# Seven products for eight in four row pairs of a down projection

## The chip, the cores and the metric

The kernel runs on one core of a Trainium2 chip. The metric is the device time of one execution in microseconds (us), lower is better. A core has a matrix engine (TensorE, PE in the profile; its loads of the stationary operand are the row PEld), a vector engine (VectorE, DVE), a scalar engine (ScalarE, ACT), a general engine (GpSimd, POOL) and the queue SP, from which most transfers are issued. Each engine runs its instructions in the order in which they were written, and semaphores make it wait for others.

## The reference

One decoder layer on x (512 tokens by 1024): a token mixer, then a gated MLP with a convolution, each followed by a residual sum and a layer norm. The change lies in the last third, the down projection of the MLP and the layer norm behind it:

```python
def conv_ffn(h, w_up, conv_w, conv_b, w_down):
    u = causal_dwconv(h @ w_up, conv_w, conv_b)
    g, val = jnp.split(u, 2, axis=-1)
    return (jax.nn.silu(g) * val) @ w_down          # 512 x 2816 times 2816 x 1024
# in reference():
        y = conv_ffn(h, w_up, conv_w, conv_b, w_down)
        x = layer_norm(DEEPNORM_ALPHA * x + (1.0 + g2) * y, ln2_g, ln2_b)
```

All is float32. `g2` is a row of 1024 gate values, computed from the conditioning vector c.

## The kernel before, in words

**Precision.** Every large product is made from three: a float32 operand is split into a high part (rounded to the matrix engine's faster float32 form, by a copy on ScalarE) and a low part (the rest, by a subtraction on VectorE), and `mm3` (line 464) adds high x high, high x low and low x high into one bank of the accumulation memory. So each weight tile and each activation tile needs one ScalarE copy and one VectorE subtraction before TensorE may use it.

**Order.** The kernel is written as threads (Python generators) that yield operations, buffers (`buf`, `bank`) and conditions (`Need`). A planner, class `Order`, keeps a clock for each engine and a model price for each operation (`price`, line 199); it emits, engine by engine, the operation that can start first, and among those that can start at about the same time the one with the lowest priority number. What it emits is a fixed order for each engine; on the chip only data and buffers make engines wait. Buffers come in classes: `b` (25 of 4 KB per partition: raw weights, their parts, most middle rows), `e` (6 of 8 KB), `h` (2 of 16 KB), `s` (9 of 2 KB) and `ps` (the 8 accumulation banks, 512 columns each). `R.limit` caps how many of a group may be held at once; all instructions are recorded at line 316, where the planner emits them.

**The up projection** already uses seven products for eight in its tiles 2 to 21 (`seven`, line 729, tiles `sP`). It ends at the mark `fin` (line 1826).

**The down projection** (`ffn`, from line 1823) has two halves of 512 output columns. Half n runs over 22 rows of 128 middle values, taken as 11 row pairs; `by_tile` (line 1674) takes one weight item (a row pair, 128 x 2 x 512) after the other, and for each the four token tiles. For each of the two rows and each token tile there is one `mm3` with 128 tokens of a middle row as the stationary operand and 512 columns of weights as the moving one. Half 0 has four accumulation banks; half 1 has five, since the last token tile is cut in two. The last item of half 0 and the last five of half 1 are run tile by tile, so that layer norm can begin with the first tile.

**What feeds it.** `w_load` (line 742) issues the weight loads on SP, at most 3 raw items at a time after `fin`. `w_split` (line 764) splits each into `wh` and `wl`; at most 8 such buffers (group `w2`) are held. The last 11 items, those of half 1, are first multiplied by the gate row (`raw<-raw,RW`, lines 769 to 772), which half 0 gets later, in `ln2`. The priority of `w_split` depends on how many items it is ahead of TensorE (`split_pri`, line 796). `keep` (line 1452) splits middle rows 6 to 21, which the up projection left unsplit in the buffers `KEEP`, into the tiles `MID`; rows 12 to 19 lie in two buffers of class e, the others by pairs in class b. When those two buffers are free, `x_back` (line 1324) loads the normalized rows XN back from memory, and `row_loads` (line 1479) scales them on GpSimd, a multiplication and an addition for each of 8 half rows, for the residual sum.

**Layer norm** (`ln2`, line 1500) runs per token tile: for half 0, the bank times the gate row, added to XN; for half 1, the bank added to XN; then statistics, the normalization, and the stores.

Of the kernel before, what the change touches and what calls it, by code (L numbers as in the profile page):

```python
# [107 lines left out]
class Order:  # L108
# [90 lines left out]
    def price(self, eng, fn, outs, ins, kw):  # L199
# [221 lines left out]
def layer_kernel(  # L421
# [247 lines left out]
    def start_h():  # L669
        for k in range(KC):  # L670
# [69 lines left out]
    RAW, W, wpos, lead = {}, {}, [0, 0], [0.0, 0.0]  # L740

    def w_load():
        yield Need("loads")
# [11 lines left out]
    def sums_seven(j, r1, a11, a21):  # L755
# [5 lines left out]
        QS[j] = q  # L761
        R.mark(("qs", j))

    def w_split():
        yield Need(("hk", KC - 1))
        for i, (shape, _) in enumerate(items):
            yield Need(("raw", i))
            raw = RAW.pop(i)
            if i >= len(items) - NFF // 2:
                yield Need("g2p")  # L770
                g2 = RES["rw"][:, 0, None, HS[1]].to_broadcast([P, 2, 512])
                yield V.tensor_mul(raw, raw, g2)
            if 0 <= i - len(items) + LATE_DN < 2:
                yield Need("fin")
                m = 2 * (i - len(items) + LATE_DN)
                hi, lo = RES["w"][:, m], RES["w"][:, m + 1]
            elif UP0 <= i < UP0 + 2 * NFF and (i - UP0) // 2 in SEVEN:
                if (i - UP0) % 2 == 0:
                    yield Need(("raw", i + 1))
                    yield from split_seven((i - UP0) // 2, raw, RAW[i + 1])  # L780
                R.free(raw)
                wpos[1] = i + 1
                continue
            else:
                own = i >= UP0 + NSPLIT
                hi = yield buf("b", shape, "wh", "w2" if own else "wh", F32R)
                lo = yield buf("b", shape, "wl", "w2" if own else "wl", F32R)
            yield A.activation(hi, raw, AF.Copy)
            yield V.tensor_sub(lo, raw, hi.bitcast(F32))
            R.free(raw)  # L790
            W[i] = (hi, lo)
            wpos[1] = i + 1
            lead[1] += 1
            R.mark(("w", i))
# [657 lines left out]
    def keep():  # L1452

        yield Need("tsused")
        for j in (12, 16):
            KEEP[j] = yield buf("e", [P, 4, SEQ], "keep")
            R.mark(("keep", j))
        yield Need("fin")
        for j in range(NMID, NFF):
            if 12 <= j < 20:  # L1460
                if j % 2 == 0:
                    E8[j] = yield buf("e", [P, 2, 2, SEQ], "mid2", dt=F32R)
                mid = E8[j - j % 2][:, j % 2]
# [6 lines left out]
            R.mark(("mid", j))  # L1470
            n = 4 if 12 <= j < 20 else 2
            if j % n == n - 1:
                R.free(KEEP[j - j % n])
                R.mark(("kfree", j - j % n))
# [4 lines left out]
    def row_loads():  # L1479
# [18 lines left out]
        R.free(*lt, *ab)  # L1498

    def ln2(t, ps, cuts):  # L1500
# [170 lines left out]
    LATE = 4  # L1671
    LATE_DN = 5

    def by_tile(tiles, total, late, block, key, after=None):

        w = {}
        for i in range(total):
            if i < total - late:
                need, n_ = w_next()
                yield Need(need)  # L1680
                w[i] = W.pop(n_)
                for t in tiles:
                    yield from block(i, t, w[i])
                R.free(*w.pop(i))
                if after:
                    after(i)
# [100 lines left out]
    def ffn():  # L1787
# [37 lines left out]
        RES["w"] = yield buf("h", [P, 4, 2, 512], "wlast", dt=F32R)  # L1825
        R.mark("fin")
        R.limit(gemm=8, raw=3, w2=8)
        ps = {}
        cuts = [[(0, 512), (512, DM)]] * 3 + [[(0, 512), (512, 768), (768, DM)]]
        for n in range(2):  # L1830
            for t in range(NT):
                for c in cuts[t][1:] if n else cuts[t][:1]:
                    ps[t, c[0]] = yield bank("gemm", "dn")
                if n == 0:
                    R.spawn(ln2(t, ps, cuts[t]), 0.5 if t == NT - 1 else 1)

            def block(i, tile, w):
                t, (c0, c1) = tile
                s, c = slice(t * P, (t + 1) * P), slice(c0 - n * 512, c1 - n * 512)
                for b in range(2):  # L1840
                    k = 2 * i + b
                    yield Need(("mid", k))
                    yield mm3(ps[t, c0][:, :c1 - c0], MID[k][:, 0, s], MID[k][:, 1, s],
                              w[0][:, b, c], w[1][:, b, c], k == 0, k == NFF - 1)

            tiles = [(t, c) for t in range(NT) for c in (cuts[t][1:] if n else cuts[t][:1])]
            yield from by_tile(tiles, NFF // 2, (1, LATE_DN)[n], block, lambda tile: ("y2", tile[0], tile[1][0]))

    def ada_last():
        yield Need(("item", UP0 - 12))  # L1850
# [30 lines left out]
    R.spawn(products(), lambda: 0.4 if ("hh", 0) in R.done and "b0" not in R.done else 9)  # L1881
    R.spawn(w_load(), 5)
    R.spawn(w_split(), split_pri)
    R.spawn(ada_mid(), lambda: 3 if wpos[0] > 16 else 8)
    R.spawn(ffn_params(), 8)
    R.spawn(x_rows(), 6)
# [36 lines left out]
```

## Time and profile before

| | before |
|---|---|
| median of 3 runs | 689.41 us (689.15 to 689.91) |
| the profiled execution | 689.18 us |
| its span, first to last instruction | 687.5 us |
| mean granted clock of TensorE | 0.998 of full speed |
| TensorE busy | 677.6 us of the span |
| down projection on TensorE | 556.65 to 679.50 us |
| VectorE busy, ScalarE busy, GpSimd busy | 596.7, 389.3, 111.8 us |

The span runs from the first to the last instruction of one execution; its own time is 1.68 us longer. A row of a timeline gives the start, the duration, the engine, the line, the operation, output<-inputs and the number of instructions merged; in square brackets stands how long the engine was idle before it and what it waited for. Matmuls overlap: one of 512 columns is shown with about 0.39 us, while the next starts earlier. Their spacing is read from the starts. A row of a group gives the count, the busy time and the mean duration in ns, and behind the bar the idle time before it.

### The profile page before, as it was taken

The page shows a single profiled execution, that of the slowest core. Times are in us where ns is not written, and L with a number is a line of the kernel's source. Part 1 is how long each engine was busy: PE and PEld are TensorE (multiplying, and loading weights), DVE is VectorE, ACT ScalarE, POOL GpSimd, SP SyncE. Part 2 cuts the span into 40 slices and gives each one's busy share as a digit, 9 for nine tenths or more (in the row PEclk, how much of TensorE's full clock was granted, in tenths as well). Part 3 has the DMA queues.
Part 4 walks back from the last instruction along what each step waited for, and adds up shares of the span by engine and source line. Part 5 has one row for each costly group of instructions (what it writes and reads, how often), then busy time and mean ns, then how long its engine had stood idle before and what let it go on. Part 6 is the DMA issues. An engine that isn't in the chain of part 4 may idle for free.

```text
span 687.5 us, 11745 instructions
## 1 busy us (share of the span) xinstructions
PE 677.6 (99%) x4400; PEld 595.5 (87%) x4400; DVE 596.7 (87%) x1069; ACT 389.3 (57%) x749; POOL 111.8 (16%) x112
## 2 busy tenths in 40 slices
PE   9999999999999999999999999999999999999995
PEld 8887878888878788787999999999999988888884
DVE  4989999999989999796889999999999997467655
ACT  4666877564665552333887777777777784212200
POOL 0020122000100001002202212212222006900022
PEclk9999999999999999999999999999999999999999
DMA  9993762245456367748659778688889467322212
GB/s 299 369 276 117 230 191 67 57 129 182 127 139 214 115 220 271 258 159 219 173 135 207 188 157 197 155 186 190 166 184 213 137 216 232 105 92 85 69 37 88
DMA packets 130441, 117.70 MB, mean 171 GB/s; under 512 B 6724, under 2 KB 108880, under 8 KB 130384
## 3 DMA queue, kind: packets, MB, share of 16 engines
q1 hardware_dynamic: 116863, 106.44, 49.9%
q0 software_dynamic: 13440, 10.49, 10.6%
q8 instruction: 34, 0.56, 0.3%
q14 instruction: 24, 0.19, 0.1%
q10 hardware_dynamic: 80, 0.03, 0.0%
HBM read 107.45 MB, written 4.24 MB: 162 GB/s over the span
## 4 chain that ended last, share of the span: by engine, by line
PE 94%; DVE 3%; ACT 2%; issue 0%; POOL 0%; DVEq 0%; ACTq 0%; POOLq 0%
PE sP L316 27%; PE fm L316 18%; PE dn L316 18%; PE po L316 10%; PE first L316 6%; PE tm L316 3%; PE psS L316 1%; PE pov L316 1%; PE pT L316 1%; PE py L316 1%; PE up L316 1%; DVE wq L316 1%; PE pst L316 1%; PE pyo L316 1%; DVE u L316 1%; PE pa L316 1%
## 5 line engine op out<-in xcount | busy, mean ns | idle before, releaser
L316 PE MATMUL sP<-ts,wq 128*128 128x256 f32 x960 | 120.2, 281 | 0.3 <-ACT c L316 0.2
L316 PEld LDWEIGHTS sP<-ts,wq 128*128 128x128 f32 x960 | 116.2, 189 | 0.7 <-ACT c L316 0.7
L316 DVE TENSOR_TENSOR wl<-raw,wh 128x1024 fp32r<-128x1024 f32 x62 | 79.3, 1284 | 34.0 <-ACT wh L316 33.2
L316 ACT ACTIVATE wh<-raw 128x1024 fp32r<-128x1024 f32 x62 | 65.1, 1054 | 75.4 <-PE dn L316 31.1
L316 PE MATMUL dn<-wh,mid 128*128 128x512 f32 (+1 forms) x356 | 102.7, 371 | 0.0
L316 PE MATMUL sP<-h2h,wq 128*128 128x256 f32 x480 | 91.2, 280 | 0.0
L316 PEld LDWEIGHTS sP<-h2h,wq 128*128 128x128 f32 x480 | 76.4, 189 | 0.0
L316 PEld LDWEIGHTS dn<-wh,mid 128*128 128x128 f32 x356 | 64.6, 188 | 12.6
L316 PE MATMUL fm<-hh,wh 128*128 128x512 f32 x176 | 73.3, 416 | 0.0
L316 PE MATMUL fm<-hl,wh 128*128 128x512 f32 x176 | 69.3, 394 | 0.0
L316 PE MATMUL fm<-hh,wl 128*128 128x512 f32 x176 | 69.3, 394 | 0.0
L316 PE MATMUL sP<-h2l,wq 128*128 128x256 f32 x240 | 67.2, 280 | 0.0
L316 PE MATMUL dn<-wl,mid 128*128 128x512 f32 (+1 forms) x178 | 66.0, 371 | 0.0
L316 DVE TENSOR_TENSOR wq<-raw,wq 128x512 fp32r<-128x512 f32 x80 | 53.5, 685 | 0.0
L316 ACT ACTIVATE wq<-raw 128x512 fp32r<-128x512 f32 x80 | 47.8, 626 | 0.0
L316 PEld LDWEIGHTS sP<-h2l,wq 128*128 128x128 f32 x240 | 45.3, 189 | 0.0
L316 ACT ACTIVATE wq<-sw 128x512 fp32r<-128x512 f32 x60 | 37.1, 626 | 11.6 <-DVE sw L316 11.3
L316 PE MATMUL po<-wh,os 128*128 128x512 f32 x128 | 41.4, 395 | 0.0
L316 ACT ACTIVATE c<-sP 128x256 f32<-128x256 f32 x80 | 30.6, 382 | 19.0 <-PE sP L316 18.5
L316 DVE TENSOR_TENSOR wq<-sw,wq 128x512 fp32r<-128x512 f32 x60 | 40.9, 684 | 0.0
L316 PEld LDWEIGHTS fm<-hh,wh 128*128 128x128 f32 x176 | 33.2, 188 | 8.0 <-issue 2.0
L316 POOL DMA_DIRECT2D sw<-in_ffn_up_w_dram x20 | 26.6, 1330 | 82.9 <-DVE u L316 46.0
(263 smaller groups left out, 1448.3 us busy)
## 6 DMA issues: line engine op xcount, KB each, us to landing
raw<-in_ffn_up_w_dram SPq DMA_DIRECT2D x44, 512.0 KB
raw<-in_mix_in_w_dram SPq DMA_DIRECT2D x26, 512.0 KB
ad<-in_ada_w_dram SPq DMA_DIRECT2D x24, 512.0 KB
raw<-in_ffn_down_w_dram SPq DMA_DIRECT2D x22, 512.0 KB
raw<-in_mix_out_w_dram SPq DMA_DIRECT2D x12, 512.0 KB
sw<-in_ffn_up_w_dram SPq DMA_DIRECT2D x20, 256.0 KB
raw<-raw POOLq DMA_DIRECT2D x20, 256.0 KB, 4.2
sw<-in_ffn_up_w_dram POOLq DMA_DIRECT2D x20, 256.0 KB, 5.7
```

The lines of the kernel that those rows point to most:

```text
L316: getattr(self.hw[op.eng], op.fn)(*op.args, **op.kw)
```

## The change

**Four row pairs of half 0.** The weight items of half 0 come in a new order of rows, 0, 2, 4, 6, 12, 8, 14, 16, 10, 18, 20. Pairs 12, 14, 16 and 18 are computed by seven products of halves (tokens by 256, one row, columns by 256) where there were eight. For this, `w_split` also makes four sums of the quarter weights (`tsum`) and splits them (`th`, `tl`); `keep` makes four sums of the middle rows in place and splits them (`sm`), into a new buffer `sh` of class h for pairs 12 and 14, into four buffers of class s for 16 and two of class b for 18. The sums shared between outputs collect in four more banks (`dP`), which `zero` clears with ScalarE; `other` issues the products, and after the last set `collapse` copies the four banks to memory (SBUF) on ScalarE and combines them with eight additions on VectorE.

**ln2** then adds these shared sums (`CX`) to the bank, multiplies by the gate row, and adds to XN: one VectorE instruction more for each token tile in half 0.

**The gate's products** of half 1 leave `w_split` for a thread of their own, `w_scale`, with a slightly lower priority number; it may be up to three items ahead.

**The residual.** The scaling of XN waits for the fourth set of weight sums (`dt7`). Its 8 additions on GpSimd become 8 accumulating DMAs issued from GpSimd. The buffer `wlast` is taken when `sh` is given back. The planner's model price of a GpSimd tensor operation is raised, and it treats the banks `dP` and `dn` as one piece.

```diff
-        self.regs[t.tensor.name].whole = a.name == "sP"
+        self.regs[t.tensor.name].whole = a.name in ("sP", "dP", "dn")
...
-        return 0.1 + 0.0022 * n
+        return 0.16 + 0.0026 * n
...
+    KO = ([0, 2, 4, 6, 12, 8, 14, 16, 10, 18, 20], list(range(0, NFF, 2)))
...
-        for k in range(0, NFF, 2):
+        for k in KO[n]:
             rows_item(w_dn, k, n)
+    DS = {12: 'h0', 14: 'h1', 16: 's', 18: 'b'}
...
+    def w_scale():
+        for i in range(len(items) - NFF // 2, len(items)):
+            yield Need(("raw", i), "g2p", ("w", i - 3))
+            raw = RAW[i]
+            yield V.tensor_mul(raw, raw, RES["rw"][:, 0, None, HS[1]].to_broadcast([P, 2, 512]))
+            R.mark(("scaled", i))
...
     def w_split():
...
+            if 0 <= i - DS0 < NFF // 2 and KO[0][i - DS0] in DS:
+                q = raw.rearrange("p k (h c) -> p (k h) c", h=2)
+                s = yield buf("b", [P, 4, 256], "tsum", "w2")
+                yield V.tensor_add(s[:, 0:2], q[:, 0:4:3], q[:, 1:2].to_broadcast([P, 2, 256]))
+                yield V.tensor_add(s[:, 2], s[:, 0], q[:, 3])
+                yield V.tensor_add(s[:, 3], s[:, 2], q[:, 2])
+                th = yield buf("b", [P, 4, 256], "th", "w2", F32R)
+                tl = yield buf("b", [P, 4, 256], "tl", "w2", F32R)
+                yield A.activation(th, s, AF.Copy)
+                yield V.tensor_sub(tl, s, th.bitcast(F32))
+                R.free(s)
+                W[i] = (hi, lo, th, tl)
...
     def keep():
...
+            if j - 1 in DS:
+                x0, x1 = KEPT[j - 1], KEPT[j]
+                yield V.tensor_sub(x1[:, H], x0[:, H], x1[:, H])
+                yield V.tensor_sub(x0[:, H], x0[:, L], x0[:, H])
+                yield V.tensor_sub(x0[:, L], x1[:, H], x0[:, L])
+                yield V.tensor_add(x1[:, L], x1[:, L], x0[:, L])
...
+                if parts:
+                    src = KEEP[j - j % n][:, j % n - 1:j % n + 1] if (n := 4 if 12 <= j < 20 else 2) else 0
+                    yield A.activation(parts[0], src, AF.Copy)
+                    yield V.tensor_sub(parts[1], src, parts[0].bitcast(F32))
...
     def row_loads():
...
+        yield Need("dt7")
         for row in lt + ab:
             yield A.activation(row, row, AF.Copy, scale=ALPHA)
...
                 yield G.tensor_mul(xn, xn, lt[n])
-                yield G.tensor_add(xn, xn, ab[n])
+                yield GD.dma_start(xn, ab[n], accum_op=OP.add)
...
     def ln2(t, ps, cuts):
...
-                y = yield buf("s", [P, c1 - c0], "y2")
-                yield V.tensor_mul(y, ps[t, c0][:, :c1 - c0], g2p[:, c0:c1])
+                yield Need(("col", t))
+                y = CX.pop(t)
+                yield V.tensor_add(y, ps[t, c0], y)
                 R.free(ps[t, c0])
+                yield V.tensor_mul(y, y, g2p[:, c0:c1])
                 yield V.tensor_add(q, q, y)
...
     def ffn():
...
+            def other(i, w):
...
+                for t in range(2):
+                    pa, pz = pb[2 * t:2 * t + 2]
+                    for o, x, y in ((pa[:, L], a(0, 0, t), b[0]), (ps[t, 0][:, L], a(1, 0, t), b[2]),
+                                    (ps[t + 2, 0][:, L], a(1, 1, t), s[3]), (pa[:, H], z(3, t), s[0]),
+                                    (pz[:, H], z(1, t), s[1]), (pz[:, L], z(0, t), s[2]),
+                                    (ps[t, 0][:, H], z(2, t), b[3])):
+                        yield mm3(o, *x, *y, False, False, True)
...
+    def collapse(ps, pb):
+        for t in range(2):
+            x = []
+            for q in pb[2 * t:2 * t + 2]:
+                x.append((yield buf("s", [P, 512], "cp")))
+                yield A.activation(x[-1], q, AF.Copy)
+                R.free(q)
+            x, z = x
+            CX[t], CX[t + 2] = x, z
+            yield V.tensor_add(z[:, L], z[:, L], x[:, L])
+            yield V.tensor_sub(x[:, H], x[:, H], z[:, L])
+            yield V.tensor_add(z[:, L], z[:, L], z[:, H])
+            yield V.tensor_sub(z[:, H], x[:, H], z[:, H])
+            R.mark(("col", t), ("col", t + 2))
```

More of the change, by code (lines that the diff above doesn't have):

```diff
@@ L737, in layer_kernel @@
     for n in range(2):
-        for k in range(0, NFF, 2):
+        for k in KO[n]:
             rows_item(w_dn, k, n)
     RAW, W, wpos, lead = {}, {}, [0, 0], [0.0, 0.0]
+    DS = {12: 'h0', 14: 'h1', 16: 's', 18: 'b'}
+    DS0 = len(items) - NFF
+    SK, CX = {}, {}
+    DT = []
     def w_load():
@@ L769, in w_split @@
             if i >= len(items) - NFF // 2:
-                yield Need("g2p")
-                g2 = RES["rw"][:, 0, None, HS[1]].to_broadcast([P, 2, 512])
-                yield V.tensor_mul(raw, raw, g2)
+                yield Need(("scaled", i))
             if 0 <= i - len(items) + LATE_DN < 2:
-                yield Need("fin")
+                yield Need("wlast")
                 m = 2 * (i - len(items) + LATE_DN)
@@ L789, in w_split @@
             yield V.tensor_sub(lo, raw, hi.bitcast(F32))
+            W[i] = (hi, lo)
+            if 0 <= i - DS0 < NFF // 2 and KO[0][i - DS0] in DS:
[10 more added lines that the diff above has]
+                W[i] = (hi, lo, th, tl)
+                DT.append(i)
+                if len(DT) == 4:
+                    R.mark("dt7")
             R.free(raw)
-            W[i] = (hi, lo)
             wpos[1] = i + 1
@@ L1470, in keep @@
             R.mark(("mid", j))
+            if j - 1 in DS:
[4 more added lines that the diff above has]
+                yield V.tensor_add(x1[:, L], x1[:, L], x0[:, L])
+                home = DS[j - 1]
+                if home[0] == "h":
+                    if "sh" not in RES:
+                        yield Need("sh")
+                    parts = [RES["sh"][:, int(home[1]), p] for p in range(2)]
+                elif home == "b":
+                    parts = []
+                    for p in range(2):
+                        parts.append((yield buf("b", [P, 2, SEQ], "sm", "mid", F32R)))
+                else:
+                    parts = None
+                if parts:
+                    src = KEEP[j - j % n][:, j % n - 1:j % n + 1] if (n := 4 if 12 <= j < 20 else 2) else 0
+                    yield A.activation(parts[0], src, AF.Copy)
+                    yield V.tensor_sub(parts[1], src, parts[0].bitcast(F32))
+                    SK[j - 1] = [[parts[p][:, i // 2, 256 * (i % 2):256 * (i % 2) + 256] for p in range(2)] for i in range(4)]
+                else:
+                    ts = []
+                    for p in range(4):
+                        ts.append((yield buf("s", [P, SEQ], "sm", dt=F32R)))
+                    for a in range(2):
+                        yield A.activation(ts[2 * a], (x0, x1)[a], AF.Copy)
+                        yield V.tensor_sub(ts[2 * a + 1], (x0, x1)[a], ts[2 * a].bitcast(F32))
+                    SK[j - 1] = [[ts[2 * (i // 2) + p][:, 256 * (i % 2):256 * (i % 2) + 256] for p in range(2)] for i in range(4)]
+                    parts = ts
+                SK[j - 1].append(parts if home[0] != "h" else [])
+                R.mark(("sk", j - 1))
             n = 4 if 12 <= j < 20 else 2
@@ L1672, in layer_kernel, with by_tile @@
     LATE_DN = 5
-    def by_tile(tiles, total, late, block, key, after=None):
+    def by_tile(tiles, total, late, block, key, after=None, other=None):
         w = {}
@@ L1681, in by_tile @@
                 w[i] = W.pop(n_)
-                for t in tiles:
-                    yield from block(i, t, w[i])
+                if other and len(w[i]) == 4:
+                    yield from other(i, w[i])
+                else:
+                    for t in tiles:
+                        yield from block(i, t, w[i])
                 R.free(*w.pop(i))
@@ L1835, in ffn @@
                     R.spawn(ln2(t, ps, cuts[t]), 0.5 if t == NT - 1 else 1)
+            pb, left = [], [len(DS)]
+            if n == 0:
+                R.spawn(zero(pb), 2.4)
             def block(i, tile, w):
@@ L1840, in block @@
                 for b in range(2):
-                    k = 2 * i + b
+                    k = KO[n][i] + b
                     yield Need(("mid", k))
                     yield mm3(ps[t, c0][:, :c1 - c0], MID[k][:, 0, s], MID[k][:, 1, s],
-                              w[0][:, b, c], w[1][:, b, c], k == 0, k == NFF - 1)
-            tiles = [(t, c) for t in range(NT) for c in (cuts[t][1:] if n else cuts[t][:1])]
-            yield from by_tile(tiles, NFF // 2, (1, LATE_DN)[n], block, lambda tile: ("y2", tile[0], tile[1][0]))
+                              w[0][:, b, c], w[1][:, b, c], i + b == 0, i + b == NFF // 2, n == 0)
@@ new lines, in other, with a, z @@
+            def other(i, w):
+                k = KO[n][i]
+                yield Need(("mid", k), ("mid", k + 1), ("sk", k), "pz")
+                b = [[w[p][:, r, c] for p in range(2)] for r in range(2) for c in (L, H)]
+                s = [[w[2 + p][:, r] for p in range(2)] for r in range(4)]
+                def a(r, half, t):
+                    c = slice(256 * half + t * P, 256 * half + (t + 1) * P)
+                    return [MID[k + r][:, p, c] for p in range(2)]
+                def z(r, t):
+                    return [SK[k][r][p][:, t * P:(t + 1) * P] for p in range(2)]
+                for t in range(2):
[5 more added lines that the diff above has]
+                        yield mm3(o, *x, *y, False, False, True)
+                R.free(*SK[k][4])
+                left[0] -= 1
+                DS[k] = ""
+                if "w" not in RES and not any(h[:1] == "h" for h in DS.values()):
+                    R.free(RES["sh"])
+                    RES["w"] = yield buf("h", [P, 4, 2, 512], "wlast", dt=F32R)
+                    R.mark("wlast")
+                if not left[0]:
+                    R.spawn(collapse(ps, pb), 2.6)
@@ new lines, in ffn, with zero @@
+            tiles = [(t, c) for t in range(NT) for c in (cuts[t][1:] if n else cuts[t][:1])]
+            yield from by_tile(tiles, NFF // 2, (1, LATE_DN)[n], block, lambda tile: ("y2", tile[0], tile[1][0]),
+                               other=other)
+    def zero(pb):
+        for _ in range(4):
+            p = yield bank("gemm", "dP")
+            yield A.activation(p.rearrange("p (a b) -> p a b", b=P), ident[:, None, :].to_broadcast([P, NT, P]),
+                               AF.Copy, scale=0.0)
+            pb.append(p)
+        R.mark("pz")
@@ L1883, in layer_kernel @@
     R.spawn(w_split(), split_pri)
+    R.spawn(w_scale(), lambda: split_pri() - 0.1)
     R.spawn(ada_mid(), lambda: 3 if wpos[0] > 16 else 8)
```

4 lines of the change are left out of this document (2 added, 2 removed).

## The prediction

> **What bounds the kernel now.** I read the page first, then the chain that ended last over the final 148 us, then what TensorE waited for, then the windows. The page and the chain:
>
> ```profile
> span 687.5 us, 11745 instructions
> ...
> PE 677.6 (99%) x4400; PEld 595.5 (87%) x4400; DVE 596.7 (87%) x1069; ACT 389.3 (57%) x749; POOL 111.8 (16%) x112
> ```
> ```profile
> 556.65 122.85 PE dn L316 x594
> 679.50 0.02 issue
> 679.52 0.43 DVE XN L316
> 679.96 0.02 issue
> 679.98 0.44 DVE st L316
> ```
>
> TensorE is busy for 677.6 of 687.5 us. The chain of the down projection is one unbroken piece of 594 matmuls, 556.65 to 679.50; behind it stand 8.0 us of the last tile's layer norm on VectorE. TensorE's list of waits has nothing inside this stage; the one wait near it is the up projection's:
>
> ```profile
> PE sP L316 <- ACT c L316: 0.2, 1, 0.2
> ```
>
> So in this stage a matmul less is time less, and whatever makes TensorE wait is time more. The windows say how much room the other engines have there (columns: busy time and instructions of PE, PEld, DVE, ACT, POOL, then the granted clock, DMA share, GB/s):
>
> ```profile
> 500.00:520.00 20.00, 20.00 (x173) 20.00 (x171) 19.96 (x34) 14.57 (x29) 5.25 (x5) 1.00 0.84 183
> ...
> 560.00:580.00 20.00, 20.00 (x88) 16.20 (x87) 16.67 (x24) 14.29 (x23) 7.11 (x3) 1.00 0.63 222
> 580.00:600.00 20.00, 20.00 (x88) 16.14 (x87) 9.26 (x5) 3.18 (x3) 19.53 (x13) 1.00 0.39 120
> ```
>
> VectorE is idle for 3.3 us in the first of the two down windows and 10.7 us in the second. That room is what the change spends.
>
> **Term 1: the matmuls.** A row pair costs 4 token tiles x 2 rows x 3 = 24 matmuls of 512 columns; by the new function it costs 7 products x 2 token tiles x 3 = 42 of 256. Both spacings stand in TensorE's timeline:
>
> ```profile
> 549.35 4.43 PE L316 MATMUL sP<-ts,wq 128*128 128x256 f32 x36
> 553.62 0.28 PE L316 MATMUL sP<-h2h,wq 128*128 128x256 f32 x1
> ...
> 612.45 0.40 PE L316 MATMUL dn<-wl,mid 128*128 128x512 f32 x1
> ...
> 621.49 0.39 PE L316 MATMUL dn<-wl,mid 128*128 128x512 f32 x1
> ```
>
> 36 matmuls of 256 start in 553.62 - 549.35 = 4.27 us, 0.1186 each. Between the two rows of 512 lie 13 groups of three, 9.04 / 39 = 0.2318 each. So 24 x 0.2318 = 5.56 us become 42 x 0.1186 = 4.98 us, 0.58 less per pair and **2.33 less for four**. No matmul is added elsewhere: the four extra banks are zeroed by ScalarE. [...]
>
> **Term 2: is each set ready when TensorE comes?** The first half starts at 556.5. With 5.56 us for an ordinary pair and 4.98 for a new one, in the new order 0, 2, 4, 6, 12, 8, 14, 16, 10, 18, 20, the pairs end at 562.1, 567.6, 573.2, 578.8, 583.7, 589.3, 594.3, 599.2, 604.8, 609.8 and 615.3 (before: 617.7). What VectorE must do ahead of them, with durations from its timeline:
>
> ```profile
> 562.74 1.22 DVE L316 TENSOR_TENSOR wl<-raw,wh 128x1024 fp32r<-128x1024 f32 x1
> 563.88 4.48 DVE L316 TENSOR_TENSOR mid<-keep,mid 128x512 fp32r<-128x512 f32 x7
> 568.28 1.22 DVE L316 TENSOR_TENSOR wl<-raw,wh 128x1024 fp32r<-128x1024 f32 x1
> 569.41 4.90 DVE L316 TENSOR_TENSOR mid<-keep,mid 128x512 fp32r<-128x512 f32 x8
> ...
> 615.22 0.69 DVE L316 TENSOR_TENSOR XN<-XN,y 128x512 f32<-128x512 f32 x1
> 615.94 0.69 DVE L316 BATCH_NORM_STATS2 st<-XN 128x6 f32<-128x512 f32 x1
> ```
>
> Back to back, a 1024-wide subtraction takes 1.14 (562.74 to 563.88) and a 512-wide one 0.61 (4.90 / 8). A 512 with a dependent one behind it takes 0.72 (615.22 to 615.94), a dependent 256 takes 0.46 (679.52 to 679.98 in the chain above). The weight sums of one pair are 0.72 + 2 x 0.46 + 1.14 = 2.78, its activation sums 4 x 0.46 + 1.14 = 2.98: **5.76 us more VectorE per pair, 23 us for four**. By the end of pair 14 (594.3), when 16 must be ready, VectorE owes from 562.74 on: four low parts (12, 8, 14, 16: 4 x 1.14 = 4.6), twelve middle rows (12 x 0.61 = 7.3), three weight sums (8.3), three activation sums (9.0): 29.2 us in 31.5. Counted in the same way the other deadlines are looser: 11.8 in 16.0 for pair 12 (one low part, eight middle rows, one of each sum), 21 in 26.6 for 14, 38.5 in 42 for 18. It fits, but with 2.3 us to spare at 16, and the hand-overs must be hidden. One is this:
>
> ```profile
> 622.82 1.21 DVE L316 TENSOR_TENSOR raw<-raw,RW 128x1024 f32<-128x1024 f32 x1
> 625.23 1.23 DVE L316 TENSOR_TENSOR wl<-raw,wh 128x1024 fp32r<-128x1024 f32 x1 [1.21 <-ACT wh L316]
> ```
>
> VectorE idles 1.21 us from its result to ScalarE's copy to its next subtraction. A weight set goes the same way: 1.64 of additions, 1.2 of hand-over, 1.14, some 4.4 us with the semaphores. Such a gap is filled when the other thread (keep or w_split) has something ready.
>
> What sets the start is the buffers. ScalarE's splits now wait for TensorE to release weights:
>
> ```profile
> ACT wh L316 <- PE dn L316: 31.1, 7, 4.5
> ```
>
> w_split may hold 8 (limit w2=8), and a new pair takes 4 plus one for the sums, so only two pairs fit. For 14, sums and high part get theirs when 12 ends (583.7), and 4.4 us later it is ready at 588.1, ahead of 589.3. For 16, which follows 14 directly, the last of the four (tl) comes only when 14 is done: its buffer is read last five matmuls (0.6 us) before 594.3, then 1.2 us of subtraction, ready at about 595. But the first two products of pair 16 don't use the sums: 6 x 0.1186 = 0.7 us cover that, and 0.2 remain. 18 has an ordinary pair ahead of it, as 14 has. I take **+0.2 to +0.4 for term 2**; the bounds are nothing, and 5.4 (the third rival).
>
> ScalarE's durations are on the page:
>
> ```profile
> L316 ACT ACTIVATE wh<-raw 128x1024 fp32r<-128x1024 f32 x62 | 65.1, 1054 | 75.4 <-PE dn L316 31.1
> ...
> L316 ACT ACTIVATE wq<-raw 128x512 fp32r<-128x512 f32 x80 | 47.8, 626 | 0.0
> ```
>
> It gets 4 x 0.63 for zeroing, 4 x 1.05 for each kind of sum and 4 x 0.63 for reading the banks out, 13.5 us over 55; it is idle for 16.8 of 20 us in 580 to 600. What hides all of this is TensorE's own 59 us (556.5 to 615.3). The residual rows on SP's queue come when keep's buffers are free, that is behind the activation sums (I count about 582 and 597, where the trace has 568 and 574); a weight load behind them in that queue waits as long, and the loads for 16, 10 and 18 are far enough ahead (seven pairs are loaded by 553) for that to cost nothing unless rival 1 holds.
>
> **Term 3: the way into the second half.** Before, its first weights were issued at 586.93, 31 us ahead of use (617.7), by my count of the 22 loads the twelfth:
>
> ```profile
> 586.93 0.37 SPq L316 DMA_DIRECT2D raw<-in_ffn_down_w_dram  x1
> ```
>
> In the change all 25 buffers of class b are taken from about 592 on (14 middle rows, two of sums for 18, 8 weights and one raw): I find the first free one for this load at about 605, when pair 10 ends. A load of this size lands 4.6 us after its issue (first row to POOL's start below), 609.6; multiplication 1.2, ScalarE 1.06, subtraction 1.2 with gaps: 613.3, and TensorE wants it at 615.3. Cover 2.0 us. [...]
>
> ```profile
> L316 POOL TENSOR_TENSOR XN<-XN,l x16: 1283/1298/5523, 572.8 to 601.5; 128x512 f32<-128x512 f32 x16
> ```
> ```profile
> 568.25 0.94 SPq L316 DMA_DIRECT2D XN<-drxn  x2
> ```
> ```profile
> 572.82 5.52 POOL L316 TENSOR_TENSOR XN<-XN,l 128x512 f32<-128x512 f32 x1 [39.38 <-DMA XN<-drxn]
> ```
> ```profile
> 579.78 2.26 DVE L316 TENSOR_TENSOR wl<-raw,wh 128x1024 fp32r<-128x1024 f32 x1 [2.60 <-ACT wh L316]
> ```
>
> A POOL multiplication takes 1.30 alone; the one at 572.82, beside a packed VectorE, took 5.52, and a subtraction beside POOL took 2.26 for 1.22. [...] Two instructions on the way at +1.04 each give 2.1, just the cover. I take **0 to +0.2 here**, bounds 0 and 2.5. Half of POOL's work (8 additions, 10.4 us) goes to DMAs; POOL is off the path either way:
>
> ```profile
> raw<-raw POOLq DMA_DIRECT2D x20, 256.0 KB, 4.2
> ```
> ```profile
> L316 POOL DMA_DIRECT2D sw<-in_ffn_up_w_dram x20 | 26.6, 1330 | 82.9 <-DVE u L316 46.0 <-DVE sw L316 26.3 <-DVE wq L316 5.0
> ```
>
> VectorE also gets the collapse (8 x 0.46 = 3.7) and one more addition per tile in ln2 (4 x 0.68 = 2.7) around 610 to 625; one pair of the second half lasts 5.5 us of TensorE and needs 2.4 of VectorE, so this fits behind w_split's priority. The multiplications put ahead are the same 11 of 1.22; TensorE waited for none of them, so they bring nothing by themselves. The four row scalings on ScalarE (4 x 0.63) move with the residual's; on POOL nothing stands behind that wait until ln2's last part. The last 8.0 us are not touched.
>
> **Sum.** 689.18 (the profiled execution, 1.68 outside its span; the median of the runs is 689.41, so 0.23 above) - 2.33 + 0.3 + 0.15 = **687.3**.
>
> **The rivals.**
> 1. *The second half starts late.* The load at 605, +1.04 twice, or VectorE, whose queue is in order, standing in front of a residual row that its DMA has not yet landed (POOL 1.30 + 1.33 per half row, 4.2 to land), with pair 11's or 12's subtraction behind it. For it: three pairs of lead shrink to one. Against: 2.0 us of cover, and priority for weights. Price 1 to 2.5: about 688.9.
> 2. *The rows that VectorE waits for starve.* The 5.52 us row shows that POOL gets no turn beside a packed VectorE. If that happens to two of the eight multiplications, ln2's rows come 2 x 4.2 = 8.4 us late, and with one 5.5 us pair in hand the rest shows: -2.33 + 2.9 + 0.4, about 690.2; with no pair in hand it is 695.
> 3. *Slower: the sets come late.* One mechanism, at pair 16: VectorE's 29.2 us are packed, but three weight sums and three activation sums each leave 1.2 to 1.3 of hand-over, 7.7 together. With none filled, 36.9 in 31.5: 5.4 us late, 692.2. It decides from the point where more than 4.6 of the 7.7 stay open (2.3 spare plus the 2.33 of term 1). For it: keep is one thread and does nothing else while it waits. Against: w_split is another, and ready at most of these moments.
> 4. *Narrow matmuls are held by the weight loads.* PEld is busy 20.00 of 20 in the 256-column window above, and one load takes 0.189 us by itself:
>
> ```profile
> L316 PEld LDWEIGHTS sP<-ts,wq 128*128 128x128 f32 x960 | 116.2, 189 | 0.7 <-ACT c L316 0.7
> ```
> If the loads overlapped nothing, a pair would be 42 x 0.189 = 7.94, four pairs 9.5 slower, 698.7; it decides above 5.56 / 42 = 0.1325. Against: the same row's 960 loads ran in 116.2 us, overlapped. [...]
> 5. *It doesn't do what it says*: the gain is there, but eaten by another order of the planner in the same stage, 689.2.
>
> **How the numbers follow.** Forecast 0.53 (own range 686.5 to 688.0), rival 1 0.18, rival 2 0.08, rival 3 0.14, rival 4 0.02, rival 5 0.05. A measurement of this kernel can tell about 0.2%, 1.4 us, from no change. Faster (below 688.0): the forecast and the mild end of 1, 0.55. Same (688.0 to 690.8): the rest of 1, half of 2, 5 and the mild end of 3, 0.28. Slower: the rest, 0.17. The range goes from 686.4 (term 1 whole, 0.4 of scatter) to 691.2.
>
> **What would show it.** 4 x (42 - 24) = 72 more matmuls than 4400; groups of 256 columns with a spacing near 0.119 in the first half; the first half's end at 615.3 to 616; no wait of TensorE on the sums. A wait of "PE dn" on VectorE's tl near 594 would be rival 3, one near 615 on wl or wh rival 1, VectorE waiting for a DMA into XN with TensorE idle rival 2. The forecast is wrong if the 122.85 us piece doesn't shorten by about 2.

## The result, and the profile after

The changed kernel takes 693.19 us (median; 692.65 to 694.38) against 689.43 (689.15 to 689.91) before, measured side by side: ratio 1.0057, 95% interval 1.0046 to 1.0067. It is 3.8 us slower; the forecast was 2.1 us faster. The profiled execution took 692.83, its span is 691.1.

The page of the changed kernel, and TensorE's list of waits (line waited for: us in total, times, longest):

```profile
span 691.1 us, 11982 instructions
...
PE 677.6 (98%) x4472; PEld 598.5 (87%) x4472; DVE 629.5 (91%) x1118; ACT 401.8 (58%) x766; POOL 100.9 (15%) x112
```
```profile
PE dn L316 <- DVE mid L316: 2.6, 2, 1.9
PE dn L316 <- DVE tl L316: 1.4, 1, 1.4
```

The count of matmuls is the predicted one, 4400 + 72. Two lines are new among the waits: the down projection waits for a low part of the weight sums (`tl`) and twice for low parts of middle rows (`mid`), 4.0 us together. Before, it waited for nothing there. The chain of waits of the changed kernel, which was a single piece of 122.85 us before, now goes through VectorE until 615.5:

```profile
608.34 1.84 DVE wl L316
610.18 2.49 DVE mid L316
612.67 2.21 DVE cp L316
...
615.53 67.84 PE dn L316 x349
```

TensorE's timeline of the changed kernel gives the places (start, duration, ..., in brackets the idle time and its releaser):

```profile
578.72 0.28 PE L316 MATMUL dP<-wh,mid 128*128 128x256 f32 x1
...
583.67 0.40 PE L316 MATMUL dn<-wh,mid 128*128 128x512 f32 x1
...
594.16 0.28 PE L316 MATMUL dP<-wh,mid 128*128 128x256 f32 x1
...
594.87 0.28 PE L316 MATMUL dn<-th,mid 128*128 128x256 f32 x1
596.56 0.39 PE L316 MATMUL dn<-tl,mid 128*128 128x256 f32 x1 [1.41 <-DVE tl L316]
...
611.53 0.40 PE L316 MATMUL dn<-wl,mid 128*128 128x512 f32 x1
...
612.72 0.73 PE L316 MATMUL dn<-wh,mid 128*128 128x512 f32 x2 [0.80 <-DVE mid L316]
613.29 0.39 PE L316 MATMUL dn<-wl,mid 128*128 128x512 f32 x1
...
615.53 0.73 PE L316 MATMUL dn<-wh,mid 128*128 128x512 f32 x2 [1.85 <-DVE mid L316]
616.80 0.58 PE L316 MATMUL dn<-wl,mid 128*128 128x512 f32 x1
```

Pair 12 starts at 578.72, pair 8 at 583.67 and pair 16 at 594.16; forecast were 578.8, 583.7 and 594.3. Up to here all is as predicted. Then three things go wrong. By its spacing (0.12 after 594.87) the matmul of 596.56 would have come at 594.99: **1.57 us** are lost in pair 16. In pair 20, the last of the half, the matmul of 612.72 comes 0.96 late (0.23 after 611.53 is 611.76), and the one of 615.53 some **2.0** late (0.23 after 613.29 is 613.52).

The fourth loss is in no list of waits. Windows of the changed kernel (length; busy time and instructions of PE, PEld, DVE, ACT, POOL; then the granted clock, DMA share, GB/s):

```profile
612.00:616.00 4.00, 1.42 (x5) 0.91 (x6) 4.00 (x4) 0.00 (x0) 3.41 (x5) 1.00 1.00 268
616.00:620.00 4.00, 4.00 (x13) 3.15 (x12) 3.97 (x4) 1.42 (x2) 3.41 (x4) 0.60 1.10 265
620.00:624.00 4.00, 4.00 (x18) 3.21 (x18) 4.00 (x3) 1.29 (x3) 3.70 (x4) 0.97 0.95 173
```

After 2.58 us without a matmul in the first window, the second runs at a mean granted clock of 0.60: from 616.80 on, nine matmuls of 512 take 3.64 us (to 620.44) instead of 9 x 0.2318 = 2.09, **1.55 us** more. The sum, with the forecast gain of the matmuls: -2.33 + 1.57 + 0.96 + 2.0 + 1.55 = +3.75; the span grew by 691.1 - 687.5 = 3.6, the median by 3.8.

Who was late? First pair 16, in VectorE's timeline of the changed kernel, with ScalarE's copy of the same sums:

```profile
592.70 1.29 DVE L316 TENSOR_TENSOR mid<-keep,mid 128x512 fp32r<-128x512 f32 x2
594.02 1.34 DVE L316 TENSOR_TENSOR keep<-keep 128x256 f32<-128x256 f32 x3
595.28 1.22 DVE L316 TENSOR_TENSOR tl<-tsum,th 128x1024 fp32r<-128x1024 f32 x1
```
```profile
592.28 1.07 ACT L316 ACTIVATE th<-tsum 128x1024 fp32r<-128x1024 f32 x1 [1.77 <-DVE tsum L316]
```

The high part was ready at 593.35. Ahead of `tl` stood two low parts of middle rows and then three of the four sums of rows 18 and 19, which `keep` makes for a set that TensorE reads twelve us later. Then pair 20, the same engine, with ScalarE and POOL beside it:

```profile
610.11 2.56 DVE L316 TENSOR_TENSOR mid<-keep,mid 128x512 fp32r<-128x512 f32 x1
612.59 2.28 DVE L316 TENSOR_TENSOR cp<-cp,cp 128x256 f32<-128x256 f32 x1
614.80 0.68 DVE L316 TENSOR_TENSOR mid<-keep,mid 128x512 fp32r<-128x512 f32 x1
```
```profile
611.03 0.64 ACT L316 ACTIVATE mid<-keep 128x512 fp32r<-128x512 f32 x1 [0.19 <-PE dP L316]
```
```profile
610.52 1.59 POOL L316 TENSOR_TENSOR XN<-XN,l 128x512 f32<-128x512 f32 x1
612.41 0.88 POOL L316 DMA_DIRECT2D XN<-l  x1 [0.30 <-POOL XN L316]
613.03 1.55 POOL L316 TENSOR_TENSOR XN<-XN,l 128x512 f32<-128x512 f32 x1
```

The 512-wide subtraction for row 20 takes 2.56 us (0.69 alone), the 256-wide collapse instruction behind it 2.28 (0.42 in a run without POOL, below), and only then, at 614.80, comes row 21. ScalarE's high part of row 21 was ready at 611.67, so it wasn't what held it. Each of the two long instructions is about as long as one turn of POOL: a multiplication, the issue of a transfer, the next multiplication 2.5 us after the first (610.52 to 613.03).

### The profile page after: what moved, and what is told of

It reads as the page before. It is cut to its first block, busy times and chain, and to the rows that moved or that the text cites. A ratio compares the mean times of both kernels' runs of the same rounds, so it can differ in the third digit from the quotient of the medians.

```text
span 691.1 us, 11982 instructions
## 1 busy us (share of the span) xinstructions
PE 677.6 (98%) x4472; PEld 598.5 (87%) x4472; DVE 629.5 (91%) x1118; ACT 401.8 (58%) x766; POOL 100.9 (15%) x112
## 4 chain that ended last, share of the span: by engine, by line
PE 80%; DVE 14%; ACT 3%; issue 2%; DMA 0%; DVEq 0%; POOL 0%; ACTq 0%; POOLq 0%
PE sP L316 21%; PE fm L316 18%; PE dn L316 10%; PE po L316 10%; PE first L316 6%; PE tm L316 3%; DVE wq L316 3%; DVE u L316 2%; DVE wl L316 2%; DVE mid L316 2%; PE psS L316 1%; PE pov L316 1%; PE pT L316 1%; PE py L316 1%; PE up L316 1%
## 5 line engine op out<-in xcount | busy, mean ns | idle before, releaser
L316 PE MATMUL dn<-wh,mid 128*128 128x512 f32 (+1 forms) x308 | 88.5, 366 | 2.6 <-DVE mid L316 2.6
L316 DVE TENSOR_TENSOR wl<-raw,wh 128x1024 fp32r<-128x1024 f32 x62 | 77.9, 1265 | 6.1 <-ACT wh L316 5.3
L316 PEld LDWEIGHTS dn<-wh,mid 128*128 128x128 f32 x308 | 56.3, 191 | 13.2 <-DVE mid L316 3.5
L316 PE MATMUL dn<-wl,mid 128*128 128x512 f32 (+1 forms) x154 | 56.3, 366 | 0.0
L316 PEld LDWEIGHTS fm<-hh,wl 128*128 128x128 f32 x176 | 33.1, 188 | 7.8
```

The source lines that it names most:

```text
L316: getattr(self.hw[op.eng], op.fn)(*op.args, **op.kw)
```

## The experiments

**Theories.** Q, the order: VectorE's queue holds late items (`tl`, rows 20 and 21) behind items that nobody needs yet. P, POOL: the residual's scaling, which the change moved beside the collapse, holds VectorE. B, buffers: the rows get their buffers too late, whatever POOL does. G: the gate's products, a step ahead, take VectorE at the wrong time. Every edit below is against the changed kernel, and its ratio is to the kernel before on the same chip.

**The scaling later.** The residual is scaled only when row 21 is split:

```diff
     def row_loads():
-        yield Need("dt7")
+        yield Need("dt7", ("mid", NFF - 1))
```

> The residual scaling on POOL also waits for the last middle row; nothing else is touched. Port theory (VectorE's subtractions for middle rows 20 and 21 are held by POOL's multiplications, 2.56 us for 0.69, TensorE then idles 2.8 us and its clock is granted at half for 3.5 us): both waits of TensorE on the middle rows go, the clock stays whole, and of the 6.1 us lost in the changed kernel 4.5 come back (0.96 + 2.0 + 1.55): about 688.7. Buffer theory (the last rows are late because their buffers come only when pair 18 ends): row 21 is still about 0.5 to 1 us late at pair 20, and a part of the 4.5 stays: 689.5 to 692. The wait on the sums of pair 16 (1.57) stays in both.

697.69 us, ratio 1.0129 [1.0113, 1.0145], far outside both expected times. The waits for rows 20 and 21 are gone, and a longer one has come, at the first matmul that needs a collapsed bank. Its TensorE timeline and one window:

```profile
629.59 0.58 PE L316 MATMUL dn<-wh,mid 128*128 128x256 f32 x1 [7.18 <-DVE cp L316]
```
```profile
626.00:627.00 1.00, 0.00 (x0) 0.00 (x0) 1.00 (x2) 0.00 (x0) 1.00 (x2) 0.50 0.86 154
```

The second half's fifth bank comes from `collapse`, copied and added up first; POOL now stood beside that addition and the gate's products. P is supported (the stall followed POOL), and starting it a few us later is no cure. The clock fell to one half at 625.64 (a mean of 0.82 in the window 625 to 626), 3.2 us after TensorE had stopped at 622.4.

**The gate's products back in `w_split`.**

```diff
     def w_split():
...
-                yield Need(("scaled", i))
+                yield Need("g2p")
+                yield V.tensor_mul(raw, raw, RES["rw"][:, 0, None, HS[1]].to_broadcast([P, 2, 512]))
...
-    R.spawn(w_scale(), lambda: split_pri() - 0.1)
```

> The gate's products go back into the weight thread, as in the kernel before; all else as changed. Queue theory (VectorE stood 2.34 us before the first product, waiting for the weights' transfer, and everything behind it came that much later): the rows 20 and 21 come 2.3 us earlier, before POOL begins, and most of the 4.5 us at pair 20 goes: about 689. Port or buffer theory: VectorE's stand is not on the way, rows 20 and 21 are as late as they were: 692.5 to 693.5.

695.99, ratio 1.0097 [1.0080, 1.0114]: 2.8 us worse than with them ahead. New waits appear on `wl` (2.8 us in two) and on ScalarE's part of a row (1.7). G falls: beside POOL, the step ahead is worth having.

**The sums of rows 18 and 19 behind pair 16's weights.**

```diff
     def keep():
...
             if j - 1 in DS:
                 x0, x1 = KEPT[j - 1], KEPT[j]
+                if j == 19:
+                    yield Need(("w", DS0 + 7))
                 yield V.tensor_sub(x1[:, H], x0[:, H], x1[:, H])
```

> The activation sums of pair 18 wait until the weight sums of pair 16 are written, so that the three 256-wide subtractions (1.3 us) no longer stand ahead of the low part of the sums of 16 on VectorE. Queue-order theory: that low part starts at 594.0 and not 595.3, TensorE's wait of 1.57 us falls to about 0.2, the rest stays: about 691.9. Buffer theory (the low part waits for the buffer that pair 14 gives back): no change there, 693.2.

688.86, ratio 0.9994 [0.9985, 1.0004]: this one condition, called the line of order below, takes back 4.3 us, more than the 1.57 it was aimed at. The low part `tl` now starts at 593.67 and not at 595.28. TensorE's only wait in the stage is now

```profile
612.67 0.73 PE L316 MATMUL dn<-wh,mid 128*128 128x512 f32 x2 [1.64 <-DVE mid L316]
```

and the clock is 1.00 in every window of the stage. Of the 4.3, 1.6 are pair 16's, about as much is the half clock that doesn't come, and the rest a shorter wait at pair 20. Q is shown for pair 16.

**Three sets in place of four**, pair 18 the old way, pair 10 between 14 and 16:

```diff
-    KO = ([0, 2, 4, 6, 12, 8, 14, 16, 10, 18, 20], list(range(0, NFF, 2)))
+    KO = ([0, 2, 4, 6, 12, 8, 14, 10, 16, 18, 20], list(range(0, NFF, 2)))
...
-    DS = {12: 'h0', 14: 'h1', 16: 's', 18: 'b'}
+    DS = {12: 'h0', 14: 'h1', 16: 's'}
...
-                if len(DT) == 4:
+                if len(DT) == 3:
```

> Three pairs by seven products (12, 14, 16) and no longer 18; the order is 0, 2, 4, 6, 12, 8, 14, 10, 16, 18, 20, so that an ordinary pair stands ahead of each set. TensorE's own work is 3 x 0.58 = 1.75 us less than before. Buffer theory: without the two buffers for the sums of 18 and the set of 18 itself, rows 20 and 21 are early and nothing waits: about 687.7. Port theory: the residual scaling now begins about 10 us earlier, behind the third set, beside VectorE's still packed work, so waits remain somewhere in pairs 16 to 20: 689 to 692.

689.65 (ten executions, 689.05 to 693.10; the profiled one took 689.05), ratio 1.0013 [1.0002, 1.0024]. No wait on `tl` and none on rows, but 1.82 us on the fifth bank's addition, with POOL's scaling at 598 to 619 beside it. Three sets are worth 1.75 us of matmuls; in the profiled execution the wait gives as much back. It does not tell Q from P, since the order and POOL's time both moved.

**No scaling at all.** The multiplications and accumulating transfers are left out, so the residual is unscaled; everything else stays. Then the same with the line of order.

```diff
     def row_loads():
...
-                yield G.tensor_mul(xn, xn, lt[n])
-                yield GD.dma_start(xn, ab[n], accum_op=OP.add)
+                pass
```

> The changed kernel without the residual scaling on POOL: its 8 multiplications and 8 accumulating transfers are left out (the residual rows enter unscaled). POOL theory (every loss from pair 20 on, the waits on rows 20 and 21, the half clock behind them, or the late fifth bank, comes from VectorE getting only one instruction per POOL turn of about 2.5 us): TensorE waits nowhere but on the sums of pair 16, 1.57 us; 689.1 - 2.33 + 1.57 = 688.4. Volume theory (VectorE has 29 us more to do and 25 buffers, and would be late at pair 20 or at the second half's start without POOL too): waits of 1 us or more remain behind pair 18, 689 to 692.

> As the run without the residual scaling (left out again), and the activation sums of pair 18 stand behind the weight sums of pair 16, as in the earlier run of that edit. POOL theory: no wait of TensorE is left in the down projection, and the matmuls' own gain shows whole: 689.1 - 2.33 = 686.8. Volume theory: a wait remains, 688 to 690.

Without the scaling: 689.28, ratio 1.0000 [0.9991, 1.0010], 3.9 us less than the changed kernel. Its VectorE timeline at the same place:

```profile
609.62 0.68 DVE L316 TENSOR_TENSOR mid<-keep,mid 128x512 fp32r<-128x512 f32 x1
611.00 0.88 DVE L316 TENSOR_TENSOR cp<-cp,cp 128x256 f32<-128x256 f32 x2 [0.70 <-ACT cp L316]
611.92 0.42 DVE L316 TENSOR_TENSOR cp<-cp 128x256 f32<-128x256 f32 x1
612.38 0.43 DVE L316 TENSOR_TENSOR cp<-cp,cp 128x256 f32<-128x256 f32 x1
612.72 0.69 DVE L316 TENSOR_TENSOR mid<-keep,mid 128x512 fp32r<-128x512 f32 x1
```

Row 20 takes 0.68, each collapse instruction 0.42 to 0.44, and row 21 starts at 612.72 instead of 614.80, although four collapse instructions stand ahead of it, not one. What is left is a wait of 1.0 us at row 21 and the 1.3 on `tl`. P is shown for most of pair 20; what is left there is B or Q.

With both edits: 686.81, ratio 0.9963 [0.9950, 0.9976]. TensorE waits for nothing in the stage, and the chain from pair 20 on is one piece:

```profile
609.83 67.54 PE dn L316 x357
```

Against before that is 689.26 - 686.81 = 2.45 us; term 1 had said 2.33. So the two causes are the whole loss, and row 21's last 1.0 us hangs on the order too. B doesn't bind: ScalarE's copy of row 21 does wait 1.12 us there, until TensorE is through with the last set (609.75), and TensorE waits for nothing.

**Multiplications or transfers?** Only the transfers stay (the multiplications are left out), then only the multiplications (the added term is left out).

```diff
# transfers alone
-                yield G.tensor_mul(xn, xn, lt[n])
                 yield GD.dma_start(xn, ab[n], accum_op=OP.add)
# multiplications alone
                 yield G.tensor_mul(xn, xn, lt[n])
-                yield GD.dma_start(xn, ab[n], accum_op=OP.add)
```

> The changed kernel with the multiplications of the residual scaling left out; the eight accumulating transfers stay. If POOL's multiplications hold VectorE (their reads from SBUF), the 256 and 512 wide VectorE instructions beside the transfers take their 0.42 and 0.69 us, and the time is that of the run without scaling, 689.3. If issuing a transfer holds it too, those instructions still show 1 to 2 us and the time stays near 691 to 693.

> The changed kernel with the accumulating transfers left out; the eight multiplications stay, now 1.3 us one behind the other. If the multiplications are what holds VectorE, instructions of 2 us and more beside them, over some 12 us and not 20; the time lies between 689.3 and 693.2, nearer the latter. If the transfers are, 689.3.

Transfers alone: 689.72, ratio 1.0004 [0.9994, 1.0014], as without any scaling. Multiplications alone: 696.43, ratio 1.0100 [1.0082, 1.0119], worse than both together. POOL's and VectorE's rows of the first, then of the second:

```profile
609.78 7.06 POOL L316 DMA_DIRECT2D XN<-l  x8 [75.75 <-ACT l L316]
...
611.00 0.88 DVE L316 TENSOR_TENSOR cp<-cp,cp 128x256 f32<-128x256 f32 x2 [0.70 <-ACT cp L316]
```
```profile
608.95 14.88 POOL L316 TENSOR_TENSOR XN<-XN,l 128x512 f32<-128x512 f32 x8 [73.55 <-ACT l L316]
...
617.29 1.75 DVE L316 TENSOR_TENSOR mid<-keep,mid 128x512 fp32r<-128x512 f32 x1
```

Eight issues of transfers in 7.06 us leave VectorE's instructions at 0.44; eight multiplications in 14.88 us stretch 0.69 to 1.75. It is the multiplications. In the second kernel VectorE also stood 2.16 us for a weight load, with row 21 behind it; how much of the 7 us between the two kernels is that and not POOL stays open. Some of it lies elsewhere: in its profiled execution (there are two, 696.34 and 696.52) TensorE came to pair 12 at 580.48 and not at 578.72 as in the changed kernel, long before the first multiplication (608.95). A wait of 0.8 us for VectorE's `prm`, which the changed kernel doesn't have, may be a part of these 1.76 us; the rest stays open.

**The scaling in the second half.** It waits for the fourth weight item of half 1, `ln2` gives its bank back before it asks for the residual; once with the line of order in `keep`, once without.

```diff
     def row_loads():
-        yield Need("dt7")
+        yield Need("dt7", ("w", DS0 + NFF // 2 + 3))
...
     def ln2(t, ps, cuts):
-            yield Need("g2p", ("res", t))
+            yield Need("g2p", ("back", t))
...
+                yield Need(("res", t))
                 yield V.tensor_add(q, q, y)
```

> All is computed. The sums of 18 behind those of 16; the residual scaling waits until four weight items of the second half are split; layer norm adds the shared sums and gives the bank back before it needs the residual row, which it waits for just ahead of its addition to XN. POOL theory: POOL's turns then fall beside the second half, where VectorE owes 2.4 us per 5.5 us of TensorE and weights are four items ahead, so they cost nothing: about 687. Volume theory: the second half's weights fall behind (8 POOL turns take some 13 us from VectorE), 689 to 692.

> All is computed. As the run before it, but without moving the activation sums of pair 18: the residual scaling in the second half, the bank given back first. POOL theory: about 688.5, the wait on the sums of pair 16 (1.57) being all that remains. Were the rows 20 and 21 held by buffers, a wait of 0.5 to 1 us there too: 689 to 690.

691.67, ratio 1.0032 [1.0020, 1.0044], and 692.91, ratio 1.0050 [1.0033, 1.0066]. The half's end is clean in the first, and TensorE waits 3.0 us for `wl` later, at 634 to 658; the second has waits of the same sum on `wl`, pair 16's wait (1.3) and 3.4 us of half clock. By the expected times this is the volume case: eight multiplications, one per 2.5 us from 619.13 to 636.32 in the first, make VectorE late in the second half too (a subtraction for `wl` took 2.58 there for 1.22), whose weights have little to spare.

**The scaling spread over the second half.** Each of the eight multiplications waits for data, not for the planner: ScalarE copies (or scales) its row of factors anew behind one weight item each. With the line of order and `ln2` as above.

```diff
-        for row in lt + ab:
+        for row in ab:
             yield A.activation(row, row, AF.Copy, scale=ALPHA)
...
+                yield Need(("w", DS0 + NFF // 2 + (2, 3, 4, 5, 6, 7, 8, 9)[2 * t + n]))
+                yield A.activation(lt[n], lt[n], AF.Copy, scale=1.0 if t else ALPHA)
                 yield G.tensor_mul(xn, xn, lt[n])
```

> All is computed. The sums of 18 behind those of 16; layer norm gives the bank back before it needs the residual row; and the eight half rows of the residual scaling are spread: each multiplication waits for a ScalarE copy of its row that stands behind the high part of one more weight item (items 3 to 10 of the second half), so that POOL takes one turn per 5.5 us of TensorE and not one per 2.5. POOL-rate theory (in the earlier run POOL took its eight turns in 20 us, and VectorE, which owed weights, products and layer norm at the same time, fell behind): no wait of TensorE is left, 689.2 - 2.33 = 686.9. If VectorE's volume in the second half is too much as such, weights are late as in that run, 689 to 691.

> As the run before it, with the eight turns behind the items 2 to 9. POOL-rate theory: the same 686.9; if the early second half is where VectorE has no room (collapse and four tiles of layer norm at once), up to 1 us more, 687 to 688.

Behind items 3 to 10 (counted from 0): 686.82, ratio 0.9960 [0.9948, 0.9973]. Behind items 2 to 9, as in the diff: **686.64, ratio 0.9962 [0.9948, 0.9975]**. Nothing is left out in either, and both beat the kernel before, by 2.5 and 2.7 us. POOL's group and the chain of the second:

```profile
L316 POOL TENSOR_TENSOR XN<-XN,l x8: 1285/1594/2002, 616.3 to 650.0; 128x512 f32<-128x512 f32 x8
```
```profile
609.59 67.57 PE dn L316 x357
```

The same eight multiplications with the same median of 1.6 us (changed kernel: 1600 ns, 606.9 to 625.5), one per 4.8 us instead of one per 2.5, cost TensorE nothing that can be seen: its list of waits has no row in the stage. Whether rows 20 and 21 could be split earlier in VectorE's order, with the scaling left where the change put it, wasn't tried.

## Why the prediction was wrong

**Term 1 (matmuls) was right.** 42 matmuls of 256 at 0.1186: from 578.72 to 583.67 pair 12 took 4.95 us, forecast 4.98. With the waits gone the matmuls give -2.45 without the scaling and -2.71 with it spread out; forecast -2.33. Some 0.4 of either lies behind the last matmul, where 7.6 us pass and not 8.0, for which I had no term. Rival 4 is out.

**Term 2 (sets ready in time) failed at pair 16, in its size.** I had the pair, the buffers and the moment right ("ready at about 595", cover 0.7), and priced the gap at 0.2 to 0.4; it measured 1.57. The step that failed is "1.2 us of subtraction, ready at about 595": it took `tl` to start when its buffer came. It started at 595.28 and ended at 596.50, since the planner had put sums for pair 18 in front of it in VectorE's queue; with these behind it, it did start at 593.67, as I had counted. The 29.2 us count was one of throughput up to a deadline; what mattered was which item stood where. Rival 3 named this place, and its sign came (a wait on `tl` near 594), but its mechanism (5.4 us from hand-overs left open) didn't show: pairs 12 and 14 were on time, and VectorE was packed, not idle, when pair 16 waited.

**"The other deadlines are looser" failed.** I counted pairs 12, 14, 16 and 18 and never pair 20, an ordinary pair whose two rows were split last of all. Before, rows 20 and 21 had been far ahead; in the change they stand behind four sets of sums. Its two waits, 0.96 + 2.0, are the largest part of the loss, and I had no term for them.

**Term 3: "POOL is off the path either way" is the step that failed and cost most.** I took two VectorE instructions at +1.04, from the 2.26 us row, 0 to 0.2 us after cover. Measured is +1.87 (2.56 for 0.69) and +1.86 (2.28 for 0.42) on two neighbours in the queue, and not on the way into the second half but at the end of the first. By the run without it, the scaling cost 3.9 us, where I had put 0 to 0.2. Rival 2 had POOL and VectorE in contention, but with POOL the starved one; here POOL kept its turn every 2.5 us and VectorE got one instruction in between. By the runs with one half of the scaling each, it was the multiplications (1.75 for 0.69 beside them) and not the issue of transfers (0.44 and 0.69, as without).

**The gate's products** "bring nothing by themselves" was read from the kernel before, where TensorE waited for none of them. In the changed kernel, with POOL beside VectorE, having them ahead is worth 2.8 us.

**Rival 1 (the second half starts late)** didn't come. The first load of its weights was issued at 596.53, not at about 605, since buffers came free earlier than I had counted; TensorE waited for no weight of half 1. Rival 5 (the gain eaten by another order) is nearest in kind, but it named no place and ended at no change.

**The clock** was in no case of mine: 1.55 us, by which 3.0 us of waiting at pair 20 became 4.5.

So the forecast's end (687.3) is near what the change gives once two placements are mended (686.64). Its range failed because no rival had pair 20 or the clock, and the one that named pair 16 had another mechanism: their bounds came from the places that I had looked at.

## What to carry to other kernels

When work is added to an engine that was half idle, write down its queue in order up to each deadline of the bound engine, the untouched items included; a sum of durations that fits says nothing about the item that stands last. Beside POOL's multiplications of 128x512, VectorE's instructions of 0.42 and 0.69 us took up to 1.9 us more each, the short one as much as the long one; so spread such work, and tie it to data: behind one weight item each, POOL's eight multiplications came one per 4.8 us, where they had come one per 2.5. A stall of TensorE like those at pair 20 (0.96 and 2.0 us) should be priced with the half clock that may follow it, 1.55 us here.

## What the runs showed of the hardware that I had not expected

**The clock drops after short waits, and not by their length alone.** In the changed kernel 0.96 and 2.0 us of waiting with 1 us of work between them were followed by a clock of 0.50. The windows of one us at its edges:

```profile
616.00:617.00 1.00, 1.00 (x6) 0.82 (x5) 1.00 (x1) 0.00 (x0) 1.00 (x1) 0.92 1.05 258
...
620.00:621.00 1.00, 1.00 (x5) 0.77 (x5) 1.00 (x2) 0.62 (x2) 1.00 (x2) 0.87 1.12 203
```

0.92 is 0.16 us at one half and 0.87 is 0.26: from 616.84 to 620.26, 3.42 us. In the kernel with the scaling in the second half and without the line of order, one wait was enough; a row of its TensorE timeline, and its windows:

```profile
648.80 0.50 PE L316 MATMUL dn<-wl,mid 128*128 128x512 f32 x1 [1.76 <-DVE wl L316]
```
```profile
649.00:650.00 1.00, 1.00 (x4) 0.82 (x4) 1.00 (x2) 0.00 (x0) 0.00 (x0) 0.69 0.05 20
650.00:651.00 1.00, 1.00 (x3) 0.78 (x3) 1.00 (x2) 0.00 (x0) 0.00 (x0) 0.50 0.00 0
...
652.00:653.00 1.00, 1.00 (x4) 0.78 (x3) 1.00 (x2) 0.17 (x1) 0.00 (x0) 0.61 0.00 0
```

A mean of 0.69 in the first of these windows is 0.62 us at one half, so the clock fell at 649.38; in the last, 0.61 is 0.78 us, so it rose at 652.78: 3.40 us. But with the gate's products in `w_split` a longer wait had no such consequence (TensorE's timeline and a window):

```profile
627.61 0.50 PE L316 MATMUL dn<-wl,mid 128*128 128x512 f32 x1 [2.08 <-DVE wl L316]
```
```profile
628.00:632.00 4.00, 4.00 (x20) 3.29 (x19) 3.15 (x4) 1.06 (x1) 0.00 (x0) 1.00 0.64 160
```

The stretches at 0.50 were of nearly one length: 3.42 and 3.40 us above, 3.42 with the multiplications alone (619.40 to 622.82, by means of 0.70 and 0.59 in the windows at its edges), 3.42 with the gate's products in `w_split` (664.44 to 667.86, by 0.72 and 0.57), and 6.84, twice that, in the run with the scaling later, where TensorE stood for 7.18 us (625.64 to 632.48, by 0.82 and 0.76). In the changed kernel the clock fell once more behind the last matmul, at 688.52 (a mean of 0.76 in 688 to 689 and 0.50 in the next): 71.68 us after the fall at 616.84, 21 times 3.413. My estimate from these lengths and this one distance is that the clock changed only at the ends of equal steps of about 3.413 us.

I laid such steps back from the falls of each execution and added up TensorE's idle time in each (the profile's, with 0.16 for each wait, since a matmul of 512 is shown with 0.39 us and the next starts after 0.23). The steps that ended in a fall held 1.92 us for the wait of 1.76 us, 2.01 in the changed kernel (the wait at 615.53 alone; the 0.96 lies in the step before), and 1.93 with the gate's products in `w_split` (two waits at 662 to 664, clock 0.50 from 664.44). The wait of 2.08 us in that last kernel lies across the end of a step, at 626.9 (eleven steps before 664.44): 1.5 us on one side and 0.7 on the other, and no fall. So, by this estimate, the bound in the down projection of these runs lies between 1.5 and 1.92 us of idling in one step. The waits of 1.64 us (the line of order alone) and 1.82 (three sets), with a clock of 1.00 behind them, say nothing more, since no fall of theirs was read that would place the steps.

**Issuing accumulating transfers from POOL leaves VectorE alone; multiplying does not**: 0.44 us per 256-wide instruction beside eight issues in 7.06 us, against 2.28 beside the multiplications of the changed kernel, and 1.75 per 512-wide one (0.69 alone) beside back-to-back multiplications.
